# Last down unit in 256-column passes, 512-feature queries and keys, and low parts by adding DMA in a two-layer decoder trunk

## The chip, the cores and the metric

The kernel runs on one core of a Trainium2 chip. The metric is the device time of one execution in microseconds; before the change the median of 3 runs is 939.41 us (938.25 to 940.3). The engines of the core are TensorE (PE in the profile, with its weight loads as PEld), VectorE (DVE), ScalarE (ACT), GpSimd (POOL) and SyncE (SP), which here only issues DMAs.

## The reference

```
for l in range(2):
    x = x + 0.5 * swiglu(rms_norm(x, ffn1_norm[l]), gate, up, down)     # 1024 -> 2816 -> 1024
    h = rms_norm(x, mix_norm[l]) @ w_in[l]                              # 1024 -> 2304
    pool, (qm, km, vm), (qd, kd, vd), conv = split(h)
    y = [pool_mixer(pool), moba_attention(rope(qm), rope(km), vm),
         dilated_attention(rope(qd), rope(kd), vd), conv_module(conv)]  # 256 features each
    x = x + concat(y) @ w_out[l]
    x = x + 0.5 * swiglu(rms_norm(x, ffn2_norm[l]), gate, up, down)
return rms_norm(x, final_norm)
```

There are 256 tokens of 1024 features in float32. The queries and keys of both attentions have 4 heads of 64 features. The convolution module ends in a layer norm over 256 features, a gain and an offset, and a SiLU.

## The kernel before, in words

**Numbers.** Every weight and every activation that goes through a large matmul is split into a high and a low part in fp32r, and a product is three matmul terms: high by high, high by low, low by high. A weight unit of 128 x 2048 numbers is loaded in two DMAs of 512 KB into `raw` (4 buffers of half a unit), ACT copies it to `hi` (line 312, `hi<-raw`), and DVE subtracts to get `lo` (line 312, `lo<-raw,hi`). `hi` and `lo` are rings of 5 units. The function `prep` does this.

**Matmul forms.** In the feed-forward parts (`halves`) the high weights pass over the high and low activations side by side, 512 columns, and the low weights pass over the high activations, 256 columns, into the left half of the same bank. The two halves of the bank are added later, for the down projections by two DVE instructions per output chunk (`x<-dn`, line 346). The form `three` makes three passes of 256 columns into one half bank; the output projection (`wo`) uses it. Queries, keys, values and the pooling input are computed with the activations as the stationary operand (`by_tokens`: 256 columns of weights per pass; the values: 512).

**Stages.** Per layer: feed-forward 1 (22 units `mm_gu`, 16 half units `dn`), the mixer (units `mm_cg`, `mm_ca`, `qd`, `kd`, two of `v`, `qm`, `km`, `pu`, four of `wo`), feed-forward 2. In the mixer, `rope` scales the projected queries or keys on ACT, rotates them on DVE and transposes them on PE (`tr_qd`), `scores` and `softmax` give `p`, `pv` transposes `p` (`pt`), copies it (`pts`) and multiplies by the values (`pv_d`, `pv_m`). The results stand in eight tiles `mx`, each with a high part by ACT and a low part by DVE. The four `wo` units take them in the order 4 (dilated attention), 0 (pooling), 2 (`pv_m`), 6 (convolution). The convolution is 54 DVE instructions on `yv`; after it come mean (`ln<-yv`), square (`lsq`), row sums on PE (`ln<-ones`), a reciprocal root by twelve small DVE steps (`v_ln`, `y_ln`, `a_ln`), a broadcast through PE and ACT (`rb_ln`), gain and offset, tanh (`lth`) and the last product.

**Order.** The class `Plan` records every operation with an engine, a cost and its dependencies, and then writes all engines' programs in an order that it works out from these costs (a list scheduler with latest start times). The cost of a DMA in that plan is its issue plus a latency `lat`. So a changed cost or latency reorders the instructions of every engine. Each engine runs its own list strictly in order and waits on semaphores.

**End.** The last output chunk `x` is updated from the last bank by two DVE instructions, squared on ACT (`sq_fin`), summed on PE (`st_fin`), and a root, a broadcast and eight products (`xg`) lead to the output DMAs.

Of the kernel before, what the change touches and what calls it, by code (L numbers as in the profile page):

```python
# [15 lines left out]
DEPTH = 2  # L16
T = 256
KC = 8
# [34 lines left out]
ALL, BLOCKS = ((0, KC),), ((0, 4), (4, 6), (6, 7), (7, 8))  # L53
W_OUT = (4, 0, 2, 6)
# [16 lines left out]
class View:  # L71
# [23 lines left out]

    def heads(self):
        return self._then(lambda t: t.to_broadcast([128, 2, 4, t.shape[3]]))
# [166 lines left out]
def trunk(ctx: ExitStack, tc: tile.TileContext, d):  # L264
# [154 lines left out]
    units, output = [], set()  # L419
    for l in range(DEPTH):  # L420
        for w in range(2):
# [5 lines left out]
            if w == 0:  # L427
                for k in range(9):
                    units.append((d["wi"][l, k], 16))
                for k in range(4):  # L430
                    output.add(len(units))
                    units.append((d["wo"][l, k], 16))
# [53 lines left out]
    def prep():  # L486
# [7 lines left out]
        for i in range(parts):  # L494
# [7 lines left out]
            tt(b - a, "tensor_sub", o, raw, h.bitcast(F32))  # L502
# [175 lines left out]
    def ffn(l, w, nrm, after):  # L678
# [27 lines left out]
        for m in range(KC):  # L706
# [17 lines left out]
    def mix(l, nrm, after):  # L724
# [62 lines left out]
        def rope(i, j, nm, col):  # L787

            ps = by_tokens(nm)
            q = slot(i, f"{nm}t{l}")  # L790
            for t in range(2):
                A(T, q.on(t)[:, t], ps.on(t)[:, t], AF.Copy, scale=col[:, t:t + 1])
            v = q.rearrange("p t (h e) -> p t h e", h=4)
            a = work("ra", 2, [128, 2, 4, 16], f"ra_{nm}{l}")
            b = work("rb", 2, [128, 2, 4, 16], f"rb_{nm}{l}")
            tt(64, "tensor_mul", b.on(0)[:, :, :, 0:8], v[:, :, :, 8:16], sin_t[:, :, :, 0:8].heads())
            tt(64, "tensor_mul", b.on(1)[:, :, :, 8:16], v[:, :, :, 0:8], sin_t[:, :, :, 8:16].heads())
            tt(128, "tensor_mul", a, v[:, :, :, 0:16], cos_t.heads())
            tt(128, "tensor_add", v[:, :, :, 0:16], a, b)
            ps = bank("qk", 2, [128, 2, T], f"tr_{nm}{l}")  # L800
            for t in range(2):
                for c in range(2):
                    transpose(0.09, ps.on(2 * t + c)[:, c, t * 128:(t + 1) * 128], q[:, t, c * 128:(c + 1) * 128])
            out = slot(j, f"{nm}{l}")
            A(512, out, ps, AF.Copy)
            return out
# [29 lines left out]
        qd = rope(8, 14, "qd", qcol)  # L836
        kd = rope(9, 15, "kd", nrm.col)
# [3 lines left out]
        psv = [bank("mm", 4, [128, 512], f"v{l}{t}") for t in range(2)]  # L841
        vt = [flat(slot(20 + t, f"vt{l}{t}")) for t in range(2)]
        sv = [Sum(), Sum()]
        for u in range(2):
            part = take()
            for t in range(2):
                sl = slice(t * 128, (t + 1) * 128)
                for i in range(4):
                    k = u * 4 + i
                    wh, wl = part(4 * i, 4)  # L850
                    xh, xl = nrm.y[k].on(0)[:, 0, sl], nrm.y[k].on(1)[:, 1, sl]
                    sv[t].mm(0.65, psv[t], (xh, wh), (xh, wl), (xl, wh))
# [27 lines left out]
        qm = rope(8, 23, "qm", qcol)  # L880
        km = rope(9, 24, "km", nrm.col)
# [41 lines left out]
        A(512, sq, yv, AF.Square)  # L923
        sq2 = work("acc", 2, [128, T], f"lsq2{l}")
# [171 lines left out]
```

## Time and profile before

| | before |
|---|---|
| median of 3 runs | 939.41 us |
| profiled execution | 939.43 us |
| its span, first to last instruction | 937.6 us |
| PE busy | 924.9 us (99%) |
| DVE busy | 721.5 us (77%) |
| ACT busy | 563.8 us (60%) |
| POOL busy | 33.3 us (4%) |
| granted TensorE clock | 0.997 of full speed |

A busy PE only means that some matmul was in flight. The duration of one matmul in a row contains the pipeline; the rate is read from a run of them: time over count. Rows of the chain of waits give such runs.

### The profile page before, as it was taken

Reading aid. Unit: us, or ns where it says so; the run is one execution under the profiler, and the core shown is the slowest. Engines: PE = TensorE matmul, PEld = TensorE weight load, DVE = VectorE, ACT = ScalarE, POOL = GpSimd, SP = SyncE. Lnnn points to the kernel's source line nnn. Section 1 sums busy time; section 2 is a strip of 40 time slices with the busy share of each in tenths; the row PEclk is TensorE's granted clock in tenths of the full one; section 3 lists DMA queues with packets and bytes.
Section 4 is the critical chain, followed back from the end, with each engine's and each line's share of the span. In section 5 each row is a group of like instructions: output and inputs, shape, how many; then the busy total and the mean of one; then the engine's idle time right before and its main releaser. Section 6 shows DMA issues by size and latency. Waiting matters only on the chain.

```text
span 937.6 us, 15074 instructions
## 1 busy us (share of the span) xinstructions
PE 924.9 (99%) x5644; PEld 822.4 (88%) x5644; DVE 721.5 (77%) x1329; ACT 563.8 (60%) x1049; POOL 33.3 (4%) x45
## 2 busy tenths in 40 slices
PE   9999999999999999999999999999999999999996
PEld 8888888898998888888888888888988988888885
DVE  6789976679888988765778887667797888886652
ACT  7776655558576676555546565445667776565540
POOL 0000000100002000000000000011000200000010
PEclk9999999999999999999999999999999999999998
DMA  8856566762164756456765554567512576654641
GB/s 301 280 199 214 171 179 199 232 217 93 35 229 156 249 200 209 127 161 195 251 213 181 180 189 137 166 193 253 187 46 96 197 239 212 221 173 125 187 125 45
DMA packets 55210, 170.18 MB, mean 181 GB/s; under 512 B 6368, under 2 KB 8416, under 8 KB 55136
## 3 DMA queue, kind: packets, MB, share of 16 engines
q1 hardware_dynamic: 54704, 168.92, 55.9%
q8 instruction: 44, 0.72, 0.3%
q10 hardware_dynamic: 432, 0.29, 0.1%
q14 instruction: 30, 0.25, 0.1%
HBM read 168.14 MB, written 1.05 MB: 180 GB/s over the span
## 4 chain that ended last, share of the span: by engine, by line
PE 93%; DVE 3%; DMA 2%; ACT 1%; issue 1%; DVEq 0%; SPq 0%; ACTq 0%
PE mm_gu L368 50%; PE dn L368 26%; PE v L368 2%; PE wo L368 2%; PE pu L368 1%; PE qd L368 1%; PE qm L368 1%; PE kd L368 1%; PE km L368 1%; PE mm_cg L368 1%; PE mm_ca L368 1%; DMA raw<-in_gu_dram 1%; DVE lo L312 1%; DVE y_f L346 1%; DMA x<-in_x_dram 1%
## 5 line engine op out<-in xcount | busy, mean ns | idle before, releaser
L312 DVE TENSOR_TENSOR lo<-raw,hi 128x1024 fp32r<-128x1024 f32 (+3 forms) x365 | 387.7, 1087 | 63.1 <-ACT hi L312 47.3
L312 ACT ACTIVATE hi<-raw 128x1024 fp32r<-128x1024 f32 (+3 forms) x365 | 329.6, 938 | 137.3 <-PE dn L368 54.8
L368 PE MATMUL mm_gu<-y_f,hi 128*128 128x512 f32 x1408 | 332.4, 391 | 0.9 <-DVE y_f L346 0.7
L368 PEld LDWEIGHTS mm_gu<-y_f,hi 128*128 128x128 f32 x1408 | 260.7, 188 | 54.8 <-ACT hi L312 1.8
L368 PEld LDWEIGHTS mm_gu<-y_f,lo 128*128 128x128 f32 x1408 | 176.0, 191 | 4.0
L368 PE MATMUL mm_gu<-y_f,lo 128*128 128x256 f32 x1408 | 178.1, 283 | 0.0
L368 PE MATMUL dn<-h,hi 128*128 128x512 f32 x704 | 169.4, 390 | 0.0
L368 PEld LDWEIGHTS dn<-h,hi 128*128 128x128 f32 x704 | 128.7, 188 | 24.1
L312 DVE TENSOR_TENSOR t<-mm_gu,t 128x256 f32<-128x256 f32 x176 | 73.0, 421 | 49.8 <-ACT t L312 47.1
L368 PEld LDWEIGHTS dn<-h,lo 128*128 128x128 f32 x704 | 91.5, 191 | 4.3
L368 PE MATMUL dn<-h,lo 128*128 128x256 f32 x704 | 92.8, 282 | 0.0
L312 ACT ACTIVATE t<-mm_gu 128x256 f32<-128x256 f32 x176 | 64.3, 375 | 30.0 <-PE mm_gu L368 29.9
L312 ACT ACTIVATE h<-th 128x256 fp32r<-128x256 f32 x88 | 36.4, 417 | 63.2 <-DVE th L312 63.1
L312 DVE TENSOR_TENSOR t<-t,rb_f 128x512 f32<-128x512 f32 x88 | 60.2, 686 | 0.9
L312 ACT ACTIVATE th<-t 128x256 f32<-128x256 f32 x88 | 36.5, 415 | 40.3 <-DVE t L312 28.5
L346 DVE SCALAR_TENSOR_TENSOR x<-dn,x 128x256 f32<-128x256 f32 x64 | 27.0, 422 | 38.8 <-PE dn L368 38.2
L368 PE MATMUL wo<-mx,hi 128*128 128x256 f32 x256 | 48.4, 289 | 1.7 <-DVE mx L312 1.7
L346 DVE SCALAR_TENSOR_TENSOR yv<-hpad,par,yv 128x256 f32<-128x256 f32 x108 | 44.0, 478 | 0.0
L312 DVE TENSOR_TENSOR h<-th,h 128x256 fp32r<-128x256 f32 x88 | 36.8, 420 | 7.6 <-ACT h L312 6.8
L368 PEld LDWEIGHTS wo<-mx,hi 128*128 128x128 f32 x256 | 39.9, 191 | 2.3 <-DVE mx L312 2.2
L312 DVE TENSOR_TENSOR th<-th,t 128x256 f32<-128x256 f32 x88 | 36.8, 419 | 5.5 <-ACT th L312 5.1
L368 PE MATMUL wo<-mx,lo 128*128 128x256 f32 x128 | 36.2, 283 | 0.0
(209 smaller groups left out, 674.4 us busy)
## 6 DMA issues: line engine op xcount, KB each, us to landing
raw<-in_gu_dram SPq DMA_DIRECT2D x170, 512.0 KB, 4.5
raw<-in_dn_dram SPq DMA_DIRECT2D x64, 384.0 KB, 3.6
raw<-in_dn_dram SPq DMA_DIRECT2D x64, 320.0 KB, 3.0
raw<-in_wi_dram SPq DMA_DIRECT2D x36, 512.0 KB, 4.7
raw<-in_wo_dram SPq DMA_DIRECT2D x16, 512.0 KB, 3.9
raw<-in_gu_dram SPq DMA_DIRECT2D x9, 256.0 KB, 5.5
con<-in_con_dram SPq DMA_DIRECT2D x1, 932.0 KB, 7.5
x<-in_x_dram SPq DMA_DIRECT2D x3, 256.0 KB, 5.4
```

Of the source, the lines that this page charges most:

```text
L312: f(*[val(x) for x in a], **{n: val(x) for n, x in k.items()})
L346: nc.vector.scalar_tensor_tensor(out, in0=a, scalar=scalar, in1=b, op0=op0, op1=op1)
L368: nc.tensor.matmul(val(o), lhsT=val(lhsT), rhs=val(rhs), start=self.i == 0, stop=self.i == self.n - 1, skip_group_check=True)
```

## The change

There are five edits.

1. In the very last half unit of the last down projection, the high passes of 512 columns and the low passes of 256 become three passes of 256 columns (`three`) into a bank of their own, `dl`. The bank of the first half unit is added to `x` by two DVE instructions before, and `dl` by one.
2. Queries and keys of one attention are computed together: `wide` makes passes of 512 weight columns (256 of the queries, 256 of the keys) into one bank for each half of the tokens. `rope` then works on one half of the tokens with all 8 heads at a time. The weights are packed accordingly on the host.
3. For the first two of the four `wo` units of each layer, `lo` is made differently: ACT writes the negated `hi` into `lo`, and a DMA issued by POOL adds the weights from DRAM onto it (`dma_add`). DVE has no part in it.
4. In the layer norm of the convolution, the square is made by two DVE products instead of one on ACT and an addition on DVE, with four row sums on PE instead of two, and the gain and offset are applied by DVE instead of ACT.
5. The latency of a load in the plan is 1.9 instead of 0.91.

```diff
-    def dma(out, in_, cols, lat=0.91):
+    def dma(out, in_, cols, lat=1.9):
...
+    def dma_add(out, in_):
+        rec("pool", 1.2, nc.gpsimd.dma_start, [out], [], (), {"out": out, "in_": in_, "accum_op": ALU.add}, lat=6.0)
...
                 for k in range(4):
                     output.add(len(units))
+                    if k < 2:
+                        apart.add(len(units))
...
             A(b - a, h, raw, AF.Copy)
-            tt(b - a, "tensor_sub", o, raw, h.bitcast(F32))
+            if n in apart:
+                A(b - a, o, h.bitcast(F32), AF.Copy, scale=-1.0)
+                dma_add(o, src[:, a:b])
+            else:
+                tt(b - a, "tensor_sub", o, raw, h.bitcast(F32))
...
+                if nm == f"{DEPTH - 1}1_{KC - 1}" and h == 1:
+
+                    for e in range(2):
+                        stt(T, x[m], ps[:, e * T:(e + 1) * T], 0.5, x[m], ALU.mult, ALU.add)
+                    ps, s = oldest(f"dl{nm}"), Sum()
+                    for i in range(FC // 2):
+                        three(s, ps[:, 0:T], part(i), hh[k0 + i])
+                    stt(T, x[m], ps[:, 0:T], 0.5, x[m], ALU.mult, ALU.add)
+                    after(m)
+                    return th
...
+        def wide(nm):
+
+            ps = [bank("mm", 4, [128, 512], f"{nm}{l}{t}") for t in range(2)]
+            sm = [Sum(), Sum()]
+            for u in range(2):
+                part = take()
+                for t in range(2):
+                    sl = slice(t * 128, (t + 1) * 128)
+                    for i in range(4):
+                        y = nrm.y[u * 4 + i]
+                        wh, wl = part(4 * i, 4)
+                        xh, xl = y.on(0)[:, 0, sl], y.on(1)[:, 1, sl]
+                        sm[t].mm(0.68, ps[t], (xh, wh), (xh, wl), (xl, wh))
+            return ps
...
-        qd = rope(8, 14, "qd", qcol)
-        kd = rope(9, 15, "kd", nrm.col)
+        qd, kd = rope(8, 14, "d")
...
-        A(512, sq, yv, AF.Square)
-        sq2 = work("acc", 2, [128, T], f"lsq2{l}")
-        tt(T, "tensor_add", sq2, sq[:, 0], sq[:, 1])
...
-        for t in range(2):
-            sp.mm(0.15, ps2.on("c")[:, 256 + t:257 + t], (sq2[:, t * 128:(t + 1) * 128], ones[:, 0:1]))
+        for c in range(2):
+            tt(T, "tensor_mul", sq.on(c)[:, c], yv.on(c)[:, c], yv.on(c)[:, c])
+            for t in range(2):
+                sp.mm(0.15, ps2.on("c")[:, 256 + t:257 + t],
+                      (sq.on(c)[:, c, t * 128:(t + 1) * 128], ones[:, 0:1]))
...
-            A(T, yv.on(c)[:, c], yv.on(c)[:, c], AF.Identity, bias=pcol(P_LB + 2 * l + c),
-              scale=pcol(P_LG + 2 * l + c))
+            ts(T, yv.on(c)[:, c], yv.on(c)[:, c], pcol(P_LG + 2 * l + c), pcol(P_LB + 2 * l + c), ALU.mult, ALU.add)
```

The first place is DVE's program in the mixer of the first layer, around the low parts `mx<-pv_m` that the third `wo` unit reads. Before:

```order
L312 TENSOR_TENSOR lsq_3010<-lsq_2993 128x256
L312 TENSOR_TENSOR lo_3013<-raw_0_2843,hi_3008 128x1024
L353 TENSOR_SCALAR v_ln_3026<-ln_3015 128x2
...
L312 TENSOR_TENSOR lo_3013<-raw_1_2919,hi_3008 128x1024
L312 TENSOR_TENSOR lo_3076<-raw_0_2949,hi_3021 128x1024
L312 TENSOR_TENSOR yv_2354<-yv_2354,rb_ln_3071 128x512
L312 TENSOR_TENSOR lo_3076<-raw_1_2988,hi_3021 128x1024
L312 TENSOR_TENSOR mx_3052<-pv_m_2998,mx_3052 128x256
L312 TENSOR_TENSOR mx_3059<-pv_m_3003,mx_3059 128x256
L346 SCALAR_TENSOR_TENSOR yv_2354<-lth_3104,yv_2354 128x512
```

And now, the same place:

```order
L311 TENSOR_TENSOR lo_2937<-raw_0_2855,hi_2931 128x1024
L311 TENSOR_TENSOR yv_2338<-yv_2338,ln_2935 128x512
L311 TENSOR_TENSOR lsq_2957<-yv_2338 128x256 x2
L311 TENSOR_TENSOR mx_2939<-pv_m_2920,mx_2939 128x256
L311 TENSOR_TENSOR mx_2942<-pv_m_2925,mx_2942 128x256
L355 TENSOR_SCALAR v_ln_2979<-ln_2969 128x2
...
L311 TENSOR_TENSOR lo_2937<-raw_1_2882,hi_2931 128x1024
L311 TENSOR_TENSOR yv_2338<-yv_2338,rb_ln_3017 128x512
L355 TENSOR_SCALAR yv_2338<-yv_2338,par 128x256 x2
L311 TENSOR_TENSOR lo_3041<-raw_0_2914,hi_2955 128x1024
L348 SCALAR_TENSOR_TENSOR yv_2338<-lth_3043,yv_2338 128x512
```

The two `mx<-pv_m` stand ahead of the small steps of the reciprocal root instead of behind them and three `lo`. The subtraction of the mean from `yv` (`yv<-yv,ln`), which stood before the last softmax steps, has come down to this place.

The second place is ACT's program at the end of the value projection, where the weights of the first `wo` units are prepared. Before:

```order
L312 ACTIVATE vt_2549<-v_2427,y_m_2227 128x512
L312 ACTIVATE hi_2559<-raw_0_2373 128x1024
L312 ACTIVATE hi_2559<-raw_1_2397 128x1024
L312 ACTIVATE hi_2581<-raw_0_2444 128x1024
L312 ACTIVATE hi_2581<-raw_1_2463 128x1024
L312 ACTIVATE qmt_2620<-qm_2544,qc_2255 128x256 x2
```

And now (`hi_2504` is the first `wo` unit, `hi_2546` the second, `qkmt` the scaled queries and keys of one half of the tokens):

```order
L311 ACTIVATE hi_2504<-raw_0_2308 128x1024
L311 ACTIVATE hi_2504<-raw_1_2323 128x1024
L311 ACTIVATE lo_2522<-hi_2504 128x1024 x2
L311 ACTIVATE hi_2546<-raw_0_2510 128x1024
L311 ACTIVATE lo_2557<-hi_2546 128x1024
L311 ACTIVATE qkmt_2571<-qkm_2488,qc_2246 128x256
L311 ACTIVATE qkmt_2571<-qkm_2488,y_m_2224 128x256
L311 ACTIVATE hi_2546<-raw_1_2529 128x1024
L311 ACTIVATE lo_2557<-hi_2546 128x1024
L311 ACTIVATE qkmt_2602<-qkm_2513,qc_2246 128x256
```

Four negated copies stand among the copies; each is followed by an adding DMA on POOL, which has nothing between them in its list.

The third place is DVE's program at the end. Before:

```order
L312 TENSOR_TENSOR lo_9836<-raw_1_9793,hi_9820 128x768
L346 SCALAR_TENSOR_TENSOR x_165<-dn_5_9798,x_165 128x256 x2
L346 SCALAR_TENSOR_TENSOR x_206<-dn_6_9863,x_206 128x256 x2
L346 SCALAR_TENSOR_TENSOR x_206<-dn_7_9915,x_206 128x256 x2
L353 TENSOR_SCALAR v_fin<-st_fin 128x2
```

And now:

```order
L311 TENSOR_TENSOR lo_9654<-raw_1_9611,hi_9638 128x768
L348 SCALAR_TENSOR_TENSOR x_165<-dn_5_9616,x_165 128x256 x2
L348 SCALAR_TENSOR_TENSOR x_206<-dn_6_9681,x_206 128x256 x2
L348 SCALAR_TENSOR_TENSOR x_206<-dn_7_9733,x_206 128x256 x2
L348 SCALAR_TENSOR_TENSOR x_206<-dl_7_9764,x_206 128x256
L355 TENSOR_SCALAR v_fin<-st_fin 128x2
```

The two updates from `dn_7` now read a bank that is complete half a unit earlier, and one update from `dl_7` is left behind the last matmul.

## Rows read from the trace of the kernel before

**Rows 1.** The page's first lines: the span, and each engine's busy time, share and instruction count.

```profile
span 937.6 us, 15074 instructions
PE 924.9 (99%) x5644; PEld 822.4 (88%) x5644; DVE 721.5 (77%) x1329; ACT 563.8 (60%) x1049; POOL 33.3 (4%) x45
```

**Rows 2.** The waits of PE: line waited for, us in total, times, longest.

```profile
PE wo L368 <- DVE mx L312: 1.7, 2, 0.9
PE st_fin L312 <- DVE y_fin L346: 1.2, 1, 1.2
PE st_fin L368 <- ACT sq_fin L312: 1.1, 1, 1.1
PE warm L368 <- POOL half_pi L312: 1.0, 1, 1.0
PE mm_gu L368 <- DVE y_f L346: 0.7, 2, 0.4
PE st_f L312 <- DVE y_f L346: 0.4, 1, 0.4
```

**Rows 3.** The chain that ended last, its end: start, us, what.

```profile
866.40 61.19 PE dn L368 x352
927.62 0.44 DVE x L346
...
928.60 0.42 ACT sq_fin L312
929.07 0.62 PE st_fin L368 x4
```

**Rows 4.** The same chain in the mixer of the first layer: start, us, what, and how many.

```profile
202.46 0.34 PE st_m L368 x4
...
222.96 5.68 PE v L368 x24
228.64 5.75 PE qm L368 x48
...
236.99 3.58 PE km L368 x30
...
259.50 1.07 PE wo L368 x9
```

**Rows 5.** The timelines of ACT and DVE in the rope of the dilated queries: the two scaled copies, and the last of the four rotation steps.

```profile
208.92 0.84 ACT L312 ACTIVATE qdt<-qd,qc 128x256 f32<-128x256 f32 x2 [0.66 <-PE qd L368]
...
210.39 0.29 DVE L312 TENSOR_TENSOR qdt<-ra_qd,rb_qd 128x128 f32<-128x128 f32 x1
```

**Rows 6.** The timeline of PE in the first layer: the multiplication by the values, and the start of the third `wo` unit with the idle time before it.

```profile
261.89 1.52 PE L380 MATMUL pv_m<-pts_m,vt 128*64 128x256 f32 x16
...
269.50 0.28 PE L368 MATMUL wo<-mx,hi 128*128 128x256 f32 x1
270.65 0.38 PE L368 MATMUL wo<-mx,hi 128*128 128x256 f32 x1 [0.87 <-DVE mx L312]
```

**Rows 7.** The timeline of DVE there.

```profile
264.13 0.15 DVE L353 TENSOR_SCALAR v_ln<-ln 128x2 f32<-128x2 f32 x1
...
266.08 0.16 DVE L346 SCALAR_TENSOR_TENSOR y_ln<-a_ln,y_ln 128x2 f32<-128x2 f32 x1
266.17 2.36 DVE L312 TENSOR_TENSOR lo<-raw,hi 128x1024 fp32r<-128x1024 f32 x2
268.44 0.68 DVE L312 TENSOR_TENSOR yv<-yv,rb_ln 128x512 f32<-128x512 f32 x1
269.04 1.22 DVE L312 TENSOR_TENSOR lo<-raw,hi 128x1024 fp32r<-128x1024 f32 x1
270.18 0.75 DVE L312 TENSOR_TENSOR mx<-pv_m,mx 128x256 fp32r<-128x256 f32 x2
...
272.69 0.75 DVE L346 SCALAR_TENSOR_TENSOR mx<-yv,mx 128x256 fp32r<-128x256 f32 x2
```

**Rows 8.** The timeline of ACT there.

```profile
261.91 3.89 ACT L312 ACTIVATE hi<-raw 128x1024 fp32r<-128x1024 f32 x4
265.69 0.65 ACT L312 ACTIVATE mx<-pv_m 128x256 fp32r<-128x256 f32 x2
267.17 0.39 ACT L312 ACTIVATE rb_ln<-ln 128x256 f32<-128x256 f32 x1 [0.83 <-PE ln L312]
...
270.29 0.63 ACT L312 ACTIVATE lth<-yv 128x512 f32<-128x512 f32 x1
```

**Rows 9.** The timelines of ACT, DVE and PE at the start of feed-forward 2 of the first layer.

```profile
277.36 2.20 ACT L312 ACTIVATE hi<-raw 128x1024 fp32r<-128x1024 f32 x2 [1.06 <-DMA raw<-in_gu_dram]
...
278.45 1.23 DVE L312 TENSOR_TENSOR lo<-raw,hi 128x1024 fp32r<-128x1024 f32 x1 [0.89 <-ACT hi L312]
279.59 1.41 DVE L312 TENSOR_TENSOR x<-wo,x 128x256 f32<-128x256 f32 x4
...
283.78 1.43 PE L368 MATMUL mm_gu<-y_f,hi 128*128 128x512 f32 x5 [0.38 <-DVE y_f L346]
```

**Rows 10.** The timelines of ACT and PE some 15 us later.

```profile
297.05 1.06 ACT L312 ACTIVATE hi<-raw 128x1024 fp32r<-128x1024 f32 x1 [3.11 <-DMA raw<-in_gu_dram]
...
300.92 0.43 PE L312 MATMUL st_f<-ident,y_f 128*128 128x128 f32 x2 [0.42 <-DVE y_f L346]
```

**Rows 11.** DMA issues of the `wo` weights: engine that issues, count, size, median us from issue to landing.

```profile
raw<-in_wo_dram SPq DMA_DIRECT2D x16, 512.0 KB, 3.9
```

More of the change, by code (lines that the diff above doesn't have):

```diff
@@ L53 @@
 ALL, BLOCKS = ((0, KC),), ((0, 4), (4, 6), (6, 7), (7, 8))
+APART = ()
 W_OUT = (4, 0, 2, 6)
@@ L416, in trunk @@
         Sum().mm(0.4, warm[:, 0:128], (mean_w, mean_w))
-    units, output = [], set()
+    units, output, apart = [], set(), set()
     for l in range(DEPTH):
@@ L431, in trunk @@
                     output.add(len(units))
+                    if k < 2:
+                        apart.add(len(units))
                     units.append((d["wo"][l, k], 16))
@@ new lines, in rope @@
+        def rope(i, j, nm):
+            ps = wide(f"qk{nm}")
+            out = [bank("qk", 2, [128, 2, T], f"tr_{n}{nm}{l}") for n in "qk"]
+            for t in range(2):
+                qk = flat(slot(i + t, f"qk{nm}t{l}{t}"))
+                for n, col in enumerate((qcol, nrm.col)):
+                    s = slice(n * T, (n + 1) * T)
+                    A(T, qk.on(n)[:, s], ps[t][:, s], AF.Copy, scale=col[:, t:t + 1])
+                v = qk.rearrange("p (h e) -> p h e", h=8)
+                a = work("ra", 2, [128, 8, 16], f"ra_{nm}{l}{t}")
+                b = work("rb", 2, [128, 8, 16], f"rb_{nm}{l}{t}")
+                sin, cos = sin_t[:, t], cos_t[:, t]
+                tt(64, "tensor_mul", b.on(0)[:, :, 0:8], v[:, :, 8:16], sin[:, :, 0:8].to_broadcast([128, 8, 8]))
+                tt(64, "tensor_mul", b.on(1)[:, :, 8:16], v[:, :, 0:8], sin[:, :, 8:16].to_broadcast([128, 8, 8]))
+                tt(128, "tensor_mul", a, v[:, :, 0:16], cos.to_broadcast([128, 8, 16]))
+                tt(128, "tensor_add", v[:, :, 0:16], a, b)
+                for n in range(2):
+                    for c in range(2):
+                        f = n * T + c * 128
+                        transpose(0.09, out[n].on(2 * t + c)[:, c, t * 128:(t + 1) * 128], qk[:, f:f + 128])
+            res = []
+            for n in range(2):
+                res.append(slot(j + n, f"{'qk'[n]}{nm}{l}"))
+                A(512, res[n], out[n], AF.Copy)
+            return res
@@ L834, in softmax @@
             return p
-        qd = rope(8, 14, "qd", qcol)
-        kd = rope(9, 15, "kd", nrm.col)
+        qd, kd = rope(8, 14, "d")
         pd = [p for c in range(2) for p in scores(qd, kd, c, C_BD, f"d{l}", 16)]
-        psv = [bank("mm", 4, [128, 512], f"v{l}{t}") for t in range(2)]
+        psv = wide("v")
         vt = [flat(slot(20 + t, f"vt{l}{t}")) for t in range(2)]
[L843 to L852, printed above, removed]
         for t in range(2):
@@ L878, in pv @@
                 tt(T, "tensor_sub", mixl[k], ps[c], mixh[k].bitcast(F32))
-        qm = rope(8, 23, "qm", qcol)
-        km = rope(9, 24, "km", nrm.col)
+        qm, km = rope(8, 23, "m")
         pv(pd, 256, 4, 16, f"d{l}")
@@ L1053 @@
     plw = np.zeros((DEPTH, 128, 2, 128), f32)
[L1054 removed]
+    cols = [16, 17, 14, 15, 0, 1]
     for l in range(DEPTH):
```

30 lines of the change are left out of this document (6 added, 24 removed).

## The prediction

> **What bounds the kernel now.** I read the page's first lines, then the waits of PE, then the chain that ended last, and only then the timelines at the places which these name. The reader is to see first that PE is busy in 924.9 of 937.6 us while DVE has 77% and ACT 60% [rows 1]. So only two things can shorten the run: fewer or cheaper matmul passes, and the few places where PE stands still. The waits of PE are short [rows 2]: 1.7 us in two waits of the output projection for `mx`, 0.7 in two at the start of a feed-forward part for `y_f`, 0.4 in one for the row of the norm, and about 2.3 at the very end around `st_fin`. What the edits take from DVE or ACT elsewhere lies beside a busy PE and is worth nothing. All that can be won from the inner waits is 1.7 + 0.7 + 0.4 = 2.8 us, 0.3% of the time.
>
> **The change part by part.** All sums are made against the profiled execution, 939.43 us, which is within 0.02 of the median of the runs shown, 939.41; 1.8 us of it lie outside the span and I leave them as they are.
>
> *The last unit.* PE ends at 927.6 and two DVE updates of 0.44 follow each other before the square [rows 3]. Now two updates belong to a bank that is complete before the last half unit begins, and lie beside PE's last 4 us; one is left. That removes 0.44. The passes: the down projections take 61.19 / 176 = 0.348 us for a pair of 512 and 256 columns [rows 3], 11 pairs 3.82. Passes of 256 in threes take 1.07 / 9 = 0.119 [rows 4], 33 of them 3.92. Net 0.10 - 0.44 = -0.34 us. What is late next is the same square and sum as before.
>
> *Queries and keys at 512.* The columns stay the same, only the passes halve: per layer 192 of 256 become 96 of 512. A pass of 256 takes 5.75 / 48 = 0.1198, one of 512 in the same form, the values, 5.68 / 24 = 0.2367 [rows 4]. Two small ones cost 0.2396, so 96 x 0.0029 = 0.28 us go per layer, 0.55 in all. The other end: the pair of the down projections less one 256 pass leaves 0.348 - 0.119 = 0.229 for 512 columns; at that rate it would be 1.0 per layer, 2.1 in all. I take 0.55, because the values run in exactly the new form.
>
> The rope behind it moves more than it adds. The scaled copies to the end of the rotation take 208.92 to 210.68, 1.76 us, for one projection [rows 5], and the new half of the tokens has the same sizes. PE covers the first half with the 12 passes of the other half (2.84 us) and the second with nine passes of the values. After that come two copies of 512 columns on ACT, with the convolution's products ahead of them in ACT's list, and only six passes of the values, 1.4 us, stand before the scores: a thin cover. The masked attention has its thin place at the second transpose of `p_m`, since ACT's list now has one step more of another head ahead of it.
>
> *Layer norm.* Two row sums on PE cost 0.34 us (`st_m`) [rows 4]; four cost as much again, +0.34 per layer, +0.68 in all, since PE is what ends last there. The square leaves ACT, gain and offset too; no row has a DVE multiply-and-add with two column operands, so I bound it by the addition of 0.42 us of the same size on one side and by nothing on the other; it is inside the next item.
>
> *The wait for `mx<-pv_m`.* PE is ready for the third `wo` unit at 269.8 and waits 0.87 [rows 6]. `pv_m` is over at 263.4. ACT's high parts come at 265.69, behind four `hi` [rows 8], and DVE's low parts at 270.18, behind three `lo` and the small steps [rows 7]. In the new order ACT has one `hi` ahead and DVE one `lo`, the mean subtraction and two squares, about 1.1 + 0.6 + 0.8 us, so both are through near 266.5, more than 3 us before they are wanted. The 1.7 us of both layers go.
>
> What is late next is the fourth unit, whose `mx<-yv` ended at 273.44, 3 us early [rows 7]. The layer norm now begins only after `pv_m`. From the first small step to the last `mx<-yv` it took 9.3 us [rows 7]; one `lo` (1.13) and the `mx<-pv_m` (0.7) leave that stretch: 7.5. Ahead of it now stand mean, subtraction, squares, row sums and the `mx<-pv_m`, some 3.7 us, and five hand-overs between engines, some 0.7: together 11.9. PE has 90 passes of `wo` left before the fourth unit, 10.7 us, and 1.8 of the norm's own small matmuls: 12.5. The margin is 0.6 us, and I cost the wait at nothing; every microsecond by which this is wrong is paid twice.
>
> *The starts of the feed-forward parts.* DVE stood idle 0.89 for a `hi` that ACT could not make for want of its load, and `x<-wo`, next in its list, began only at 279.59 [rows 9]; later ACT stood 3.11 us for a load with the row of the norm queued behind it [rows 10]. Loads land after 3.9 us [rows 11], the plan believed 0.91; with 1.9 it sets two `lo` fewer between the last `mx` and `x<-wo`. I take both waits as gone, 0.7 + 0.4 = 1.1.
>
> *Low parts by adding DMA.* It takes two units of `lo`, four instructions a layer, from DVE and gives ACT four; ACT is busy 60% [rows 1]. The DMA waits on POOL, and only the next add and much later the norm's additions stand behind it. For the first unit ACT's copies stand ahead of the scaled queries in its list, which come when PE has 12 passes of `qkm` left. From there PE has 2.8 of these, 5.7 of `pu` and about 1.5 of `pv_d` (as `pv_m` [rows 6]), at least 10 us. A plain load of that size lands in 3.9, two of them in 7.8 even one behind the other [rows 11]: covered, cost nothing. The trace has no adding DMA and none from POOL. If adding moves every byte twice, two take 15.6, 5.6 late: 11 us in both layers. That is the upper bound; the lower is nothing. I take nothing, from the nearer row.
>
> The Trainium skill speaks against this edit: SBUF — State Buffer, section "SBUF: two separate sides", says that a DMA issued by GpSimd starves for descriptors while VectorE runs an instruction in a two-port mode, and gives 3.1 us instead of 0.62. By that rule, as an estimate, each add could start 2.5 us later; the sum would still be the same, since two such delays in turn stay near the cover, and DVE's convolution steps in this stretch have two tensor inputs. No row here shows it.
>
> *New short waits.* For the thin covers named above (scores, `p_m`, the fourth unit) I add 0.6 us; they can be 0 to 2.
>
> Sum: -0.34 - 0.55 + 0.68 - 1.7 - 1.1 + 0.6 = -2.4 us, so 937.0.
>
> **The rivals.**
> *The wait only moves* from the third to the fourth unit, or to the scores. For it: a margin of 0.6 us, and three `lo` still stand in the norm's chain on DVE, each waiting for a `hi`. Against it: the order frees DVE of two units before. At 1 us per layer the time is 937.0 + 2 = 939.0, no change.
> *The adds land late* (slower). Place: the first pass of the first `wo` unit, which needs `lo`. It decides from where a pair of adds takes more than 10 us; at 15.6 it costs 5.6 per layer and the time is 937.0 + 11 = 948; at 13 it is 943. For it: the trace has no add and no DMA of POOL to judge by; against it: 3.9 us for the same bytes as a plain load [rows 11].
> *The new order harms the feed-forward parts*, which now run without any wait: 1.9 for a load is still half of what rows show, and other lists could starve PE. Half a microsecond in each of the four parts and none of the gain at their starts: 937.0 + 2 + 1.1 + 1 = 941. Against it: a larger latency puts less, not more, behind late loads.
> *512 columns run at the faster rate* of the down projections: 937.0 - 1.5 = 935.5. Against it: the values do not.
>
> **How the numbers follow.** Forecast 0.58, the moved wait 0.22, late adds 0.09, harmed order 0.05, faster rate 0.06. The likeliest time is 937.0. The forecast's own range is 936.2 (no new waits and a little of the faster rate) to 938.2 (2 us of them). The range of 8 in 10 takes in the moved wait and part of the faster rate and of the harmed order: 935.4 to 940.4. About 0.2%, 1.9 us, can be told from no change: faster means below 937.5. That takes 0.51 of the forecast's 0.58 and the faster rate: 0.57. Slower than 941.3 are the late adds and about all of the harmed order, with something for what I have not seen: 0.14. The rest, 0.29, is no change.
>
> **What would show each step.** The chain's end has one update `x<-dl` of 0.44 after PE, and PE's end to the last instruction is 0.4 shorter. `qkd` and `qkm` take 0.237 a pass, 11.4 a pair. The waits of PE no longer list `wo` for `mx<-pv_m`; if they list `wo` for `mx` by `yv`, or `qk_d` for ACT, the wait has moved. If they list `wo` for a DMA on `lo`, the adds are late, and their landing time stands in the list of DMA issues. `mm_gu` for `y_f` and `st_f` are gone from the waits. The forecast is wrong if PE's idle time inside the span does not fall by some 2 us, or if a stretch of a feed-forward part, such as the 61.2 us of a down projection, gets longer.

## The result and the profile after

The changed kernel takes 943.86 us (943.31 to 947.22, 5 runs) beside 939.82 for the kernel before: a ratio of 1.0056 (95% interval 1.0042 to 1.0069). It is 4 us slower; 2.4 us faster was forecast. Its profiled execution took 944.85 us, with a span of 943.1.

The page's first lines, to be read beside [rows 1]:

```profile
span 943.1 us, 14737 instructions
PE 926.3 (98%) x5471; PEld 817.2 (87%) x5471; DVE 717.2 (76%) x1328; ACT 570.0 (60%) x1051; POOL 39.5 (4%) x53
```

PE is busy 1.4 us more although it has 173 instructions less, and the span is 5.5 longer: time went both into standing still and into slower matmuls. The waits of PE tell where, to be read beside [rows 2]:

```profile
PE qk_m L382 <- DVE mx L311: 6.6, 2, 3.7
PE st_fin L311 <- DVE y_fin L348: 1.2, 1, 1.2
...
PE st_fin L370 <- ACT sq_fin L311: 0.7, 1, 0.7
PE pt_d L311 <- ACT pts_d L311: 0.5, 1, 0.5
PE mm_gu L370 <- DVE y_f L348: 0.2, 1, 0.2
```

The old waits of `wo` for `mx` are gone, and a larger one stands in the first row, once per layer: 2.9 and 3.7 us. A place with a wait is best priced by its whole stretch, from a first matmul to the next (`mm_cg` opens a mixer, `mm_gu` a feed-forward part; the rest holds feed-forward 2 of the second layer and the tail). In us, from PE's timeline:

| | before | after | difference |
|---|---|---|---|
| up to the first mixer | 191.14 | 190.79 | -0.35 |
| mixer, layer 1 | 91.01 | 94.28 | +3.27 |
| feed-forward 2, layer 1 | 185.80 | 184.12 | -1.68 |
| feed-forward 1, layer 2 | 184.15 | 184.15 | 0 |
| mixer, layer 2 | 90.96 | 95.56 | +4.60 |
| rest | 194.6 | 194.2 | -0.4 |
| span | 937.6 | 943.1 | +5.5 |

So nothing was lost outside the mixers, and the mixers lost 7.9 us. (The first row lies between 190.8 and 192.9 us in the traces of this document, so its -0.35 says nothing.) What ACT did in the first mixer, from its timeline:

```profile
243.54 0.87 ACT L311 ACTIVATE pts_d<-pt_d 128x384 f32<-128x384 f32 x2
246.07 1.06 ACT L311 ACTIVATE hi<-raw 128x1024 fp32r<-128x1024 f32 x1 [1.66 <-DMA raw<-in_wo_dram]
249.90 1.06 ACT L311 ACTIVATE hi<-raw 128x1024 fp32r<-128x1024 f32 x1 [2.77 <-DMA raw<-in_wo_dram]
250.86 0.64 ACT L311 ACTIVATE mx<-pv_d 128x256 fp32r<-128x256 f32 x2
```

PE ended `pv_d` at 246.8, but its copy `mx<-pv_d`, the input of the first `wo` unit, stands in ACT's list behind four `hi` of the third and fourth `wo` units (two of them are in the rows above); the last two wait 1.66 and 2.77 us for their loads. DVE's half of `mx` follows at 251.26, and PE continues:

```profile
251.74 1.15 PE L382 MATMUL qk_m<-km,qm 64*128 64x128 f32 x6 [2.93 <-DVE mx L311]
```

What PE waits for here are the scores `qk_m`, which do not read `mx` at all. In the kernel the attention's products take three of PE's eight result banks in turn, and the bank that the second head's scores are due to get is that of `pv_d`: it comes free only when ACT and DVE have read `pv_d` into `mx`. So a late copy holds up PE before the first `wo` unit is reached.

The loads are late because of what runs beside them, and because there are more of them at once. SP's issues of the `wo` loads in the first layer, before and now:

```profile
212.45 47.67 SPq L312 DMA_DIRECT2D raw<-in_wo_dram  x8
...
210.63 27.92 SPq L311 DMA_DIRECT2D raw<-in_wo_dram  x8
```

The adds read the weights from DRAM, not from `raw`, so a `raw` buffer of the first two units is free as soon as ACT has read it, and the loads of the third and fourth unit follow at once: they are issued from 231.9 to 238.2 instead of from 249.4 to 259.8, and meet the four adds, issued from 233.1 to 239.6. The list of DMA issues, to be read beside [rows 11] (median us from issue to landing):

```profile
raw<-in_wo_dram SPq DMA_DIRECT2D x16, 512.0 KB, 6.4
lo<-in_wo_dram POOLq DMA_DIRECT2D x8, 512.0 KB, 13.5
```

The adds land after 13.5 us where a plain load took 3.9, and the median of the plain `wo` loads went from 3.9 to 6.4. The last load of the fourth unit, for which ACT waits 2.77 us, stands in the chain with 11.66 (in the second layer it is 12.40):

```profile
238.22 11.66 DMA raw<-in_wo_dram
```

A view by stretches (PE, PEld, DVE, ACT and POOL busy, then granted clock, DMA share and GB/s) shows the rest of the loss:

```profile
238.00:246.00 8.00, 7.97 (x69) 7.36 (x69) 7.80 (x22) 6.38 (x12) 0.86 (x1) 1.00 1.06 279
246.00:251.00 5.00, 2.81 (x25) 2.17 (x20) 0.88 (x3) 2.16 (x3) 0.00 (x0) 1.00 1.04 220
251.00:254.00 3.00, 2.26 (x11) 1.70 (x12) 2.74 (x10) 1.66 (x6) 0.00 (x0) 0.72 0.09 16
254.00:257.00 3.00, 3.00 (x28) 2.44 (x28) 1.86 (x12) 2.00 (x10) 0.00 (x0) 0.72 0.00 0
```

From 238 to 251 the DMA engines are full (share about 1), and yet move only 279 and then 220 GB/s. After PE has stood, the granted clock falls: 0.72 over the six microseconds from 251 to 257, and 0.50, the lower level of 1.2 GHz, from 252.5 to 255.5. That is 6 x 0.28 = 1.7 us of matmul time, lost behind a wait of 2.9. In the second layer the granted clock is 0.75 and 0.68 in the two stretches of 3 us after the wait, 1.7 us again. A wait of this size costs more than its row says.

The chain's pieces for the other steps, to be read beside [rows 3] and [rows 4]:

```profile
205.51 8.18 PE qkd L370 x36
...
266.51 1.06 PE ln L370 x4
...
269.36 0.79 PE ln L370 x8
...
872.03 57.33 PE dn L370 x330
...
929.37 3.97 PE dl L370 x33
...
933.36 0.43 DVE x L348
```

A 512-column pass of `qkd` takes 8.18 / 36 = 0.227 us. The row sums of the convolution's norm are eight matmul records where four were, and cost 0.79, so the change adds about 0.4. Behind the last matmul one update is left.

### The profile page after: what moved, and what is told of

Its sections match the earlier page's. It is cut to its first block, busy times and chain, and to the rows that moved or that the text cites. A ratio compares the mean times of both kernels' runs of the same rounds, so it can differ in the third digit from the quotient of the medians.

```text
span 943.1 us, 14737 instructions
## 1 busy us (share of the span) xinstructions
PE 926.3 (98%) x5471; PEld 817.2 (87%) x5471; DVE 717.2 (76%) x1328; ACT 570.0 (60%) x1051; POOL 39.5 (4%) x53
## 3 DMA queue, kind: packets, MB, share of 16 engines
HBM read 172.33 MB, written 1.05 MB: 184 GB/s over the span
## 4 chain that ended last, share of the span: by engine, by line
PE 90%; DMA 5%; ACT 2%; DVE 1%; issue 1%; DVEq 0%; SPq 0%; ACTq 0%
PE mm_gu L370 52%; PE dn L370 26%; PE wo L370 5%; DMA raw<-in_wo_dram 4%; PE qkd L370 2%; PE mm_cg L370 1%; PE mm_ca L370 1%; DVE yv L348 1%; ACT s_d L311 1%; DMA x<-in_x_dram 1%; PE qk_m L382 1%; ACT hi L311 0%; PE v L370 0%; PE dl L370 0%; PE ln L370 0%
## 5 line engine op out<-in xcount | busy, mean ns | idle before, releaser
L311 DVE TENSOR_TENSOR lo<-raw,hi 128x1024 fp32r<-128x1024 f32 (+3 forms) x357 | 378.2, 1083 | 67.2 <-ACT hi L311 50.7
L370 PE MATMUL dn<-h,hi 128*128 128x512 f32 x693 | 166.8, 390 | 0.0
L370 PEld LDWEIGHTS dn<-h,hi 128*128 128x128 f32 x693 | 126.7, 188 | 23.7
## 6 DMA issues: line engine op xcount, KB each, us to landing
lo<-in_wo_dram POOLq DMA_DIRECT2D x8, 512.0 KB, 13.5
```

The source lines that it names most:

```text
L311: f(*[val(x) for x in a], **{n: val(x) for n, x in k.items()})
L370: nc.tensor.matmul(val(o), lhsT=val(lhsT), rhs=val(rhs), start=self.i == 0, stop=self.i == self.n - 1, skip_group_check=True)
```

## The experiments

The kernel before ran beside each group: 939.63, 938.97, 939.47 and 939.38 us. Ratios are to it, with 95% intervals.

**The adds alone undone.** DVE makes all low parts again:

```diff
-                    if k < 2:
-                        apart.add(len(units))
```

> The change without the adding DMAs: the low parts of all wo units are made by DVE again, edits 1, 2, 4 and 5 stay. Theory A (the adding DMAs are the whole loss): PE's wait of 2.9 to 3.7 us per layer ahead of wo goes, and with it the stretch at half clock; the time is 937 us, 2 to 3 below before. Theory B (the wide queries and keys or the layer norm on DVE cost the time): the wait stays near mx or yv and the time stays at 942 to 944.

942.3 us, ratio 1.0028 (1.0015 to 1.0042). Theory A falls: taking the adds out does not give the time back, and the mixers take 94.76 and 92.53 us. PE now waits for DVE and ACT in other places (`pt_m` for `yv` 2.4, `psp` for `pl` 1.7, `wo` for `lo` 1.1).

**The adds with few bytes, in the same order.** Each add moves 64 of its 1024 columns, so most of these low parts is left out; everything else, also every engine's list, is that of the changed kernel:

```diff
-                dma_add(o, src[:, a:b])
+                dma_add(o[:, 0:64], src[:, a:a + 64])
```

> The change with every instruction in its order, but each adding DMA moves 64 of its 1024 columns, so the low parts of two units per layer are left mostly unfinished. Theory A1 (the bytes of the adds hold up the plain loads on the same DMA engines, and ACT, which stands in its list at a hi for such a load, comes late to mx): plain wo loads land in 4 to 5 us again, no wait of PE for mx, 937 to 938 us. Theory A2 (it is the order: four hi stand ahead of mx in ACT's list and their loads are issued late whatever else moves): the wait of 3 us per layer stays, 942 to 944 us.

934.45 us, ratio 0.9943 (0.9929 to 0.9956), 2.5 us under what A1 expected; the mixers take 89.14 and 89.13 us. So the order is good and the bytes of the adds cost 943.86 - 934.45 = 9.4 us. The plain `wo` loads still land after 5.3 us here, not 3.9: that is the crowd of loads without the bytes of the adds. Against the run without adds this one is 7.9 us faster. There DVE makes these low parts and every list has another order; the two were not separated.

**The same bytes copied, not added**, again in the same order (`lo` then holds the whole weights instead of the low parts):

```diff
-{"out": out, "in_": in_, "accum_op": ALU.add}
+{"out": out, "in_": in_}
```

> The change with every instruction in its order, but POOL's DMAs copy the weights into lo instead of adding, so the low parts of two units per layer hold the whole weights. If the addition makes the DMA slow, a copy lands in 4 to 6 us, the plain loads in 4 to 5, and the time is 937 to 939 us. If the way over POOL (or the conversion to fp32r) makes it slow, it lands in 10 us or more and the time stays at 942 to 944 us.

934.29 us, ratio 0.9943 (0.993 to 0.9956). The view by stretches for this kernel:

```profile
238.00:246.00 8.00, 8.00 (x66) 7.47 (x66) 7.91 (x23) 7.73 (x13) 0.53 (x1) 1.00 1.08 405
246.00:251.00 5.00, 5.00 (x47) 4.01 (x45) 4.46 (x18) 3.29 (x9) 0.00 (x0) 1.00 0.16 55
```

With full DMA engines the copies and loads move 405 GB/s, where the adds and loads moved 279. By 246 it is nearly over, and ACT's last `hi` ahead of `mx<-pv_d` waits 0.70 us for its load instead of 2.77:

```profile
246.46 1.06 ACT L311 ACTIVATE hi<-raw 128x1024 fp32r<-128x1024 f32 x1 [0.70 <-DMA raw<-in_wo_dram]
```

The expectation tied a landing after 10 us to 942 to 944 us, and that did not come: a copy by POOL (which converts to fp32r, as the add does) lands after 10.2 us, and the median of the plain `wo` loads is 6.4 as with the adds, yet the time is 934.29. The medians do not decide. What counts is when the fourth unit's loads land: its two loads in the first layer take 8.6 and 7.8 us beside copies, and 11.4 and 11.7 beside adds. So the time hangs on the addition; what the DMA engines do longer for an add, no run here shows.

**The loads of the third and fourth `wo` units planned later.** The adds stay; the plan believes 12 us for these loads, so their `hi` no longer stand ahead of `mx<-pv_d`:

```diff
-            dma(raw, src[:, a:b], b - a)
+            dma(raw, src[:, a:b], b - a, 12.0 if n in output and n not in apart else 1.9)
```

> The change with the latency of the loads of the third and fourth wo unit at 12 in the plan, so that ACT makes their hi after mx; the adding DMAs stay as they are. Theory A1 or A2 (ACT is held at a hi): PE's wait for mx goes, the adds still take 13 us and hurt nobody, 937 to 939 us. Rival C of the prediction (the low parts themselves land too late): PE waits at wo for the adding DMA and the time stays above 941 us.

935.26 us, ratio 0.9952 (0.9939 to 0.9965), 4.4 us faster than before with the whole computation done, and 1.7 us under what was expected. The adds still land after 13.7 us and plain loads after 6.4, but `mx<-pv_d` no longer stands behind them:

```profile
245.30 0.39 ACT L311 ACTIVATE mx<-pv_d 128x256 fp32r<-128x256 f32 x1 [1.39 <-PE pv_d L382]
```

ACT now waits for PE alone there, 1.39 us, as an engine with time to spare does. PE still waits 0.4 us per layer, for `mx<-pv_m` before the third `wo` unit. The larger latency can move other steps of the plan too, but it leaves the slow adds and loads in place. So the mechanism of the loss is shown from both sides: taking the bytes or the addition away cures it with every list unchanged, and so does taking the waiting `hi` out of the way.

**The adds alone on the kernel before** (edit 3 only, no other line changed):

> Alone on the kernel before: the low parts of the first two output units of each layer by adding DMA; rotation, norm, tail and the assumed load time of 0.91 us stay. A (13 us adds slow the plain loads behind them, and ACT stands in order at a high part ahead of the copy that the first output unit needs): slower than before also without the new order, 941 to 944 us, the adds landing after 12 to 14 us, plain loads of wo after 6, and PE waiting 1 to 3 us per layer for mx of the distance attention. B (the loss needs the new order of the mixer, where the scores come later): the two waits of 0.87 us for mx of the masked attention go, since DVE has two low parts fewer ahead of it, and nothing takes their place: 937 to 938.

941.74 us, ratio 1.0025 (1.0015 to 1.0034). The wait for `mx` of the masked attention is gone, as B says, but new ones come before `mx` of the dilated attention is even made: PE waits 1.8 us for `km` and 1.8 for `pts_d`, copies which in ACT's list stand behind `hi` that wait 1.40 and 1.88 us for `wo` loads. The adds land after 9.8 us and plain `wo` loads after 4.5, both earlier than A expected. A is right in its time and mechanism, not in the place.

**No adds, and the load time back at 0.91.**

```diff
-    def dma(out, in_, cols, lat=1.9):
+    def dma(out, in_, cols, lat=0.91):
...
-                    if k < 2:
-                        apart.add(len(units))
```

> The changed kernel without the adding DMAs and with the assumed load time back at 0.91 us (so the tail, the queries and keys at 512 and the norm alone). In the run without adds, at 1.9 us, the mixers took 94.8 and 92.5 us, for about 90.9 before. C (it is the new order of the mixer with DVE making all low parts, whatever load time the plan believes): mixers stay over 92 us and the feed-forward part behind them goes back to about 185.9: 942 to 944. D (it is the load time, which puts low parts of output units in front of the attention's steps): mixers fall to 90 to 91, with the longer feed-forward start the time is 938 to 940.

944.67 us, ratio 1.0056 (1.0041 to 1.007), mixers 94.34 and 94.95. C is right about the mixers (the feed-forward part did not get longer again: 184.12). The load time is not what makes the kernel without adds slow, and the shorter feed-forward part does not need edit 5 in the new order.

**Queries and keys at 512 alone** (edit 2 on the kernel before):

> Alone on the kernel before: queries and keys in 512-column passes with the rotation by halves of the tokens; norm, low parts, tail and the assumed load time as before. E (the wider rotation brings the scores of the masked attention so late that DVE, with all low parts to make, cannot follow: this edit is what makes the version without adds slow): PE waits for yv, pl or lo before the first output unit, mixers of 93 to 95 us, 943 to 947. F (the passes gain 0.010 us each by the measured 0.227, 0.9 a layer less 0.0 to 0.5 of new waits, and the loss needs the new norm): 937.5 to 939.

944.62 us, ratio 1.0053 (1.004 to 1.0066): one edit of the five, by itself, costs 5 us. Theory E holds in its time and its waits; its reason needs a closer look. PE's waits:

```profile
PE pt_m L312 <- DVE yv L346: 2.4, 2, 1.2
PE psp L368 <- ACT pl L312: 1.7, 2, 0.8
PE wo L368 <- DVE lo L312: 1.6, 2, 0.8
```

The scores of the masked attention do not come later: `qk_m` starts at 248.61, before at 248.89. What comes later is the convolution. Its first step on DVE, before and now, and between them ACT's list, where the convolution's products stand behind scaled copies that wait for the wide passes:

```profile
219.67 0.48 DVE L346 SCALAR_TENSOR_TENSOR yv<-hpad,par,yv 128x256 f32<-128x256 f32 x1
...
214.69 0.47 ACT L312 ACTIVATE qkdt<-qkd,qc 128x256 f32<-128x256 f32 x1 [1.88 <-PE qkd L368]
215.42 0.91 ACT L312 ACTIVATE yv<-hpad,par 128x256 f32<-128x256 f32 x2
...
224.28 0.47 DVE L346 SCALAR_TENSOR_TENSOR yv<-hpad,par,yv 128x256 f32<-128x256 f32 x1
```

Its last step ends at 255.93 instead of 247.51 (the mixer itself starts 0.6 us later in this trace). From the start of the mixer to 247.4 us DVE stands idle 10.9 us, where it was 8.4 before. Before, the convolution is over by then, and one low part of the first `wo` unit is made right behind `mx<-pv_d`:

```profile
247.43 0.79 DVE L312 TENSOR_TENSOR mx<-pv_d,mx 128x256 fp32r<-128x256 f32 x2
248.14 1.22 DVE L312 TENSOR_TENSOR lo<-raw,hi 128x1024 fp32r<-128x1024 f32 x1
```

With edit 2 alone the low parts of this unit come behind the softmax steps and the last of the convolution, when PE already wants them:

```profile
255.85 1.22 DVE L312 TENSOR_TENSOR lo<-raw,hi 128x1024 fp32r<-128x1024 f32 x1
257.06 1.20 DVE L312 TENSOR_TENSOR lo<-raw,hi 128x1024 fp32r<-128x1024 f32 x1
```

And the clock pays again, 0.79 over 8 us:

```profile
254.00:262.00 8.00, 6.01 (x35) 5.46 (x34) 7.38 (x18) 6.19 (x21) 0.00 (x0) 0.79 0.43 144
```

**The changed kernel with the load time back at 0.91, adds kept:**

```diff
-    def dma(out, in_, cols, lat=1.9):
+    def dma(out, in_, cols, lat=0.91):
```

> The changed kernel with only the assumed load time back at 0.91 us, the adds kept. Theory (high parts of output units stand in ACT's list ahead of the copy for the first output unit, and the adds make their loads late): a smaller assumed load time puts them no later, so the wait stays or grows: 943 to 948, PE waiting 6 us or more for mx in both layers. Rival (it was the larger assumed load time that brought this order): 934 to 937.

938.89 us, ratio 0.9999 (0.9988 to 1.001). Neither number: the theory's place was wrong. Here ACT waits at another `hi`, ahead of the scaled queries, and PE then waits 2.2 us in all, in both layers, before the transposes behind them:

```profile
238.31 1.06 ACT L311 ACTIVATE hi<-raw 128x1024 fp32r<-128x1024 f32 x1 [2.77 <-DMA raw<-in_wo_dram]
```

It is the same mechanism at a place where less hangs on it: what it costs depends on which step stands behind the waiting `hi`. Beside the run without adds and with the same load time (944.67, run with another group), the adds save 5.8 us here.

**The load time alone** (edit 5 on the kernel before):

> Alone on the kernel before: the plan believes 1.9 us for a load in place of 0.91. The prediction: the waits of PE for y_f (two of 0.35) and st_f (0.42) at the start of the second feed-forward part of the first layer go, all else stays: -0.7 to -1.1 us, 938.5 to 938.9. By the stretches of the changed kernel (184.1 us for that part in place of 186.0) it is 1.8: about 937.8. Rival: in the order of before the larger latency moves other steps too, and mixers change by more than 0.5 us.

938.0 us, ratio 0.9988 (0.9979 to 0.9996). Feed-forward 2 of the first layer takes 184.12 us instead of 185.80, mixers 91.02 and 90.95: the edit does what was forecast, where it was forecast, and 1.7 us by the stretch.

**The layer norm alone** (edit 4 on the kernel before):

> Alone on the kernel before: the new layer norm (squares, gain and offset on DVE, four row sums). The prediction: two row sums of 0.17 us a layer more on PE, and the waits for mx of the masked attention go in the new order: +0.68 - 1.7 = 938.0. If the norm alone does not reorder the list, the waits stay: 939.6 to 940. Rival: this edit loads DVE where it is short and makes the loss of the version without adds: 942 to 945.

938.6 us, ratio 0.999 (0.9982 to 0.9999), mixers 90.31 and 90.25. The wait for `mx` of the masked attention is gone from the list, and the edit alone is a gain of 0.7 us per mixer.

**The norm of before in the version with later loads:**

```diff
-        for c in range(2):
-            tt(T, "tensor_mul", sq.on(c)[:, c], yv.on(c)[:, c], yv.on(c)[:, c])
...
+        A(512, sq, yv, AF.Square)
...
```

> The version with the output loads planned later (935.26 us), with the layer norm of before (square, gain and offset on ACT, one DVE addition, two row sums in place of four). N1 (the sum of the prediction: two row sums less on PE, 0.34 us a layer, and ACT has room): 934.6. N2 (PE has slack at the row sums anyway, and the longer chain over ACT holds the fourth output unit): 935.3 to 938, with a wait of PE for the last mx by yv.

934.16 us (933.9 to 935.57), ratio 0.9949 (0.9937 to 0.9961). It has the lowest median of the versions that do the whole computation, but its interval overlaps that of the version with the new norm (0.9939 to 0.9965): mixer 1 gains 0.5 us and mixer 2 loses 0.3. The two cannot be told apart.

**One add per layer in place of two, in this version** (`k < 1`):

> The version with later output loads and the norm of before (934.16 us), with only the first output unit of each layer made by adding DMA, DVE making the second. If half the bytes of adds are the better share: 933 to 934, adds landing after 10 us or less. If DVE is short in the mixer, as the versions without adds show: 936 to 940, PE waiting for lo or yv before or in the first output units.

936.05 us (935.32 to 939.12), ratio 0.9968 (0.9955 to 0.9981). An add lands after 10.5 us instead of 13.9. PE waits 1.2 us in `wo`, for ACT's `mx` and not for `lo` or `yv` as the rival has it; its wait of 1.0 for `y_f` lies in the first 60 us, long before the first mixer. The two mixers take 179.7 us together in this trace and in that of the version with two adds, and the intervals of the two versions touch. No gain from half the bytes is to be seen; that they cost 1.9 us, as the medians have it, is not shown.

**Low parts by POOL, without bytes.** A subtraction on POOL in place of the negated copy and the add, in the changed kernel, in the kernel before with edit 2, and in the changed kernel with the norm of before:

```diff
-                A(b - a, o, h.bitcast(F32), AF.Copy, scale=-1.0)
-                dma_add(o, src[:, a:b])
+                gg(b - a, "tensor_sub", o, raw, h.bitcast(F32))
```

> The changed kernel with the low parts of the first two output units made by POOL as a subtraction on the chip instead of ACT's negated copy and the adding DMA: DVE is relieved of the same two units, and no byte is fetched twice. Theory (relief of DVE is what the new order needs, the adds' bytes on the DMA engines are the harm): 933 to 936, no wait of PE for mx by pv_d, plain loads of wo after 4 to 5 us. Rival (POOL takes 3 us or more for one unit and holds DVE meanwhile, or the low parts come late): 938 to 946, PE waiting for lo by POOL or for DVE's steps.

> The kernel before with queries and keys at 512 (944.62 us alone), with only the low parts of the first two output units moved to POOL. If DVE's low parts behind the convolution's steps are what makes that edit slow: mixers of 89 to 91 us, 936 to 939. If the rotation by halves brings the attention itself late, whoever makes the low parts: mixers stay at 93 or more, 943 to 946, PE waiting for yv and pl before the first output unit.

> The changed kernel with low parts of the first two output units by POOL and the norm of before. If relief of DVE without traffic is right and POOL does not slow DVE: 933 to 934.5, under the 934.16 us of the version with adds, later output loads and the norm of before. If POOL is late or holds DVE: 936 to 945.

954.64, 956.14 and 955.41 us, ratios 1.0159, 1.0181 and 1.0173 (each within 0.0018). All three lie 8.6 to 10.4 us above what the rivals allowed; the traces bear out the rival that POOL holds DVE. POOL's four subtractions of the first layer in the first of these kernels, DVE's convolution steps beside them, and the same 15 steps in the kernel without adds:

```profile
231.40 10.08 POOL L311 TENSOR_TENSOR lo<-raw,hi 128x1024 fp32r<-128x1024 f32 x4 [44.95 <-ACT hi L311]
```

```profile
231.56 14.56 DVE L348 SCALAR_TENSOR_TENSOR yv<-hpad,par,yv 128x256 f32<-128x256 f32 x15
...
231.76 6.02 DVE L348 SCALAR_TENSOR_TENSOR yv<-hpad,par,yv 128x256 f32<-128x256 f32 x15
```

Beside POOL they took 14.56 us instead of 6.02, 8.5 us more in 10.08 us of POOL's work. PE then waits 8 us per layer for the rotation behind them, in all three kernels. The Trainium skill states this: SBUF — State Buffer, section "SBUF: two separate sides", says that GpSimd and VectorE share a port pair that one of them holds for a whole instruction, and that a VectorE operation with two inputs in SBUF is blocked by a GpSimd operation that reads there. The trace agrees, with these 8.5 of 10.08 us. The runs therefore say nothing on relief without traffic; the nearest answer to that question is the run with adds of few bytes.

## Why the prediction was wrong

**The step that failed.** "A plain load of that size lands in 3.9, two of them in 7.8 even one behind the other [rows 11]: covered, cost nothing", and, between nothing and 11 us, "I take nothing, from the nearer row". The plain load was the wrong neighbour: its 3.9 us is the median of loads issued one to three at a time, and now six `wo` loads and four adds are issued within 10 us. The adds took 13.5 us each, and the first two, issued 0.9 us apart, 13.7 together, near the upper bound (two for 15.6). And the price was looked for only where `lo` is read: the adds themselves were in time even at 13.7 us, as the run with later `wo` loads shows, where no wait for an added `lo` stands. They harmed the plain loads that run at the same time, and by way of ACT's strict order the steps queued behind the copies of those loads, down to the bank that PE's next scores need: 9.4 us, where nothing was forecast. The rival that the adds land late had the right resource at the wrong place. That its sum fits (943 at 13 us) is luck: it adds 6 us of waits to 937.0, and the runs have 9.4 us on 934.4.

**The second step that failed.** "What the edits take from DVE or ACT elsewhere lies beside a busy PE and is worth nothing." With DVE making all low parts the new order is slow: 942.3 against 934.45 us with adds of few bytes. The 99% of PE belongs to one order of the lists. Edit 2 alone moved the convolution back by 4.6 us at its start and 8.4 at its end, DVE's low parts came behind it, and 5 us were gone. "Thin cover" was written against the rope, at 0 to 2 us for everything; by the runs PE of the changed kernel waits for no step of the rope, and the thin place is the low parts of the first `wo` unit and the convolution's last steps, which follow each other on DVE in the same stretch. The idle times up to there (10.9 us against 8.4) say that DVE began late rather than lacked time; no run starts the convolution earlier, so this is argued and not shown.

**Terms of the sum.**
- Tail: -0.34 forecast. Behind the last matmul the trace has one update of 0.43 in place of two, and the 33 passes took 3.97 us where 3.92 was forecast: right by its parts. The last stretch as a whole shrank by 0.4, but among the runs with this tail it lies between 194.2 and 195.1 us, so that is no proof, and this edit was not run alone.
- Queries and keys: -0.55 forecast, at the values' 0.2367 a pass. Measured 0.227: 96 x (0.2396 - 0.2272) = 1.2 per layer, -2.4 in all. The rival of the faster rate was right, and "the values do not" was a misreading of the trace of before. The row taken, 24 passes in 5.68 us, begins behind short score products, and its first pass comes 0.33 us ahead of the second; its last twelve come 0.227 apart. Another row of the same chain has twelve passes of the values at 0.229:

```profile
215.08 2.75 PE v L368 x12
```

- Row sums: +0.34 per layer; about +0.4 by the row. Right.
- The wait for `mx<-pv_m`: gone, as forecast, and also with edit 4 or edit 3 alone. The fourth unit does not wait.
- Starts of the feed-forward parts: -1.1 forecast; -1.7 by the stretch, and by edit 5 alone. Of the 1.1, 0.30 lay at the program's start, 10.7 us into the run, where [rows 9] have no say; so the rows had only 0.38 + 0.42 of what went. The rest was in passes that started late while an earlier one was still in flight, which no idle time counts. The first eight passes, before and now:

```profile
282.15 1.25 PE L368 MATMUL mm_gu<-y_f,hi 128*128 128x512 f32 x3
283.78 1.43 PE L368 MATMUL mm_gu<-y_f,hi 128*128 128x512 f32 x5 [0.38 <-DVE y_f L346]
...
285.07 2.00 PE L370 MATMUL mm_gu<-y_f,hi 128*128 128x512 f32 x8
```

  Up to the next pass they took 2.89 us before and take 1.84 now: 1.05 gone for a row of 0.38. The same at `st_f` makes 0.6 for a row of 0.42.
- New short waits: +0.6 forecast; +6.6 in the rows of the waits and 3.4 of slow clock measured, which the adds make.

With the price of the adds and of DVE's low parts taken out the sum can be tested: a mixer of before less the wait, less the faster passes, with the row sums, is 91.0 - 0.87 - 1.22 + 0.4 = 89.3 us. The run with adds of few bytes has 89.14 in both layers. So the other terms, with the measured rate of the passes, add up in this one trace.

**The rule of the Trainium skill** (SBUF — State Buffer, section "SBUF: two separate sides") that a DMA issued by GpSimd starves for descriptors while VectorE runs an instruction in a two-port mode was cited against the edit, as a late start of 2.5 us. No run here shows it: an add of 32 KB lands after 6.4 us, but plain loads of 512 KB in the same run take 5.3, and no run has an add with DVE idle. The loss came by another road.

## What to carry to other kernels

An operation that the trace does not show has no nearest row: run it once by itself, or forecast from the bad end, and ask not only when it is done but what else uses its resource meanwhile, which buffers it frees early and so which transfers it calls in, and what stands in strict order behind those. A plan that believes a load is quick puts its copy ahead of steps that are ready; where one such load shares the DMA engines with a slow transfer, tell the plan a later time for it (here 4.4 us faster than before, with the same adds). When a planner reorders everything, price each edit by whole stretches and test it alone: these edits changed the time by +5.1 us (queries and keys), +2.8 (adds), -0.9 (norm) and -1.0 (load time) by themselves (the tail was not run alone), and all five together with the loads planned later by -4.4. And a wait on PE costs more than its row of idle time: the passes around it start late too, and after a long one the granted clock falls.

## What the runs showed of the hardware

- An adding DMA of 512 KB from DRAM, issued by POOL with conversion to fp32r, lands after 9.8 to 13.9 us (medians of six kernels, beside plain loads), a plain copy of the same form after 10.2, one of 32 KB added after 6.4; a plain load by SP took 3.9 in the kernel before, 5.3 beside adds of 32 KB and 6.4 beside the adds or copies of the changed order. With the DMA engines full, adds and loads together moved 279 GB/s, copies and loads 405.
- Four POOL subtractions of 128 x 1024 (2.55 us each) held up DVE's three-operand steps for 8.5 of 10.08 us.
- A pass of 512 columns ran at 0.227 us for queries and keys and at the end of a run of the values in the kernel before. The 0.237 of [rows 4] contains the start of such a run behind short matmuls.
- After PE had stood for 2.9 us, the granted clock was 0.72 over the six microseconds from 251, 1.7 us lost; after 3.7 us in the second layer 1.7 us again.
